# A hybrid attention block on one core: high parts over 128 partitions, and an order planned with the cost of changing partitions

## The chip, the core and the metric

The kernel runs on one core of a Trainium2 chip. The core has five engines that this text names as the profile does: PE (TensorE, matrix products), DVE (VectorE), ACT (ScalarE), POOL (GpSimd) and SP (SyncE, which issues most DMAs). Each works through its own queue in order; a semaphore holds an instruction until what it reads is there. The metric is the device time of one execution in microseconds, as the median of some runs. Before the change it is 288.33 us (three runs, 288.24 to 289.02).

## The reference

One decoder block over 512 tokens of width 1024. The normalised input goes through one combined projection into four head groups of four heads with 64 dimensions: forgetting attention (f), block-sparse attention (m), stick-breaking attention (s) and sliding-window attention with sinks (w). Each group's result is gated, and all of them go through one output projection onto the residual.

```python
hn = rms_norm(x, norm_gain)
proj = jnp.einsum('btd,de->bte', hn, w_in)
...
y = jnp.concatenate([from_heads(o_fox) * jax.nn.silu(fg),
                     from_heads(o_moba) * jax.nn.silu(mg),
                     from_heads(o_sb) * jax.nn.silu(sg),
                     from_heads(o_swa) * jax.nn.silu(wg)], axis=-1)
return x + jnp.einsum('bte,ed->btd', y, w_out)
```

In f, m and w the queries and keys are normalised per head and multiplied by a gain; in s they are not.

## The kernel before, in words

All matrix products are made of float32 values split into a high part (rounded to the type that PE reads fast, fp32r) and a low part (the rest). `hi_copy` (L138) makes the high part on ACT, `lo_part` (L142) the low part on DVE. A projection then has three products per step, high x high, low x high and high x low (`mm3`, L341 to L344).

Weights come in 39 chunks of up to 128 x 1024: sv, sqk, fvf, fqk, fg, sg, mqk, mv, mg, wg, wqkv, and eight of the output projection (o0 to o7). `advance` (L222) loads a chunk (three raw buffers), makes its high part on ACT and its low part on DVE, or on POOL in pieces of at most 260 columns where its number is in `POOL_LO`.

Scores of one head need q and k with 64 dimensions on partitions. Two heads lie in one 128-row tile, head 0 on rows 0 to 63, head 1 on rows 64 to 127. `q_pair` (L416) makes for each of the two heads a 128-row tile `qs`: the high part on the head's own rows ("mine") and the low part on the other half. `k_pair` (L428) makes a tile with two blocks of columns: in the first the high part of k on both halves, in the second the low part on the head's own rows and zeros on the other half. A score is then two products with the same weights (L511 and L512, or L507 in one). For f, m and w, q and k are first transposed on PE into PSUM (`qT`, `kT`, L455); for s they come from an SBUF tile (`sqk`). In w two heads share a k (`k_shared`), which is copied over all rows.

Each head goes on through a softmax or the stick-breaking sums on DVE and ACT (`pm`), transposes of the probabilities on PE (`pT`, L524), their high and low parts (`pth`, `ptl`), the product with v (L474, L475), and `lc` and `oc`, which add the two halves of that product (L487 on ACT, L488 on DVE); `lc` moves one half of the partitions to the other. The gate is multiplied on POOL (L493), and yh and yl are the parts for the output projection.

No engine's order is written out by hand. The program is recorded in a plain order; `_plan` (L1042) then plays all instructions through with costs per instruction (`_Step.cost`), and takes, of what can start first, the one with the lowest number: its place in the program plus the numbers in `TURN` for its kind. `PATIENCE` lets an engine wait that many ns for a lower number, `MARGIN` adds to a signal's way to an engine. `order_engines` (L1118) makes each engine keep that order. So each change of a cost moves instructions on all engines.

Of the kernel before, what the change touches and what calls it, by code (L numbers as in the profile page):

```python
# [40 lines left out]

RATE, OUTU = 4.54, 0.4

POOL_LO = {1, 4, 9, 10, 12, 15, 16, 19, 21, 23, 24, 30, 32, 34, 36, 37, 39}
PIECE = 260
DVE_SQ = {(1, 1), (2, 1), (3, 0), (3, 1)}

OCUT, WARM, WARM_GAPS = 2, 3, 8


TURN = {"xn": 215, "gate": 80, "qk": -250, "v": -68, "s": 14, "pt": -264, "ot": 322, "gap":
        100000, "y": 7, "fb": 5, "w": 81, "pv": -29, "oc": 258, "nat": -5, "proj": 65, "x": -110}
PATIENCE = {"Pool": 10, "PE": 21, "Activation": 29}

MARGIN = {"PE": 100, "Activation": 52}

LEAD = {"Pool": 120, "DVE": 0}


BOUNDS = list(range(17)) + [21, 27, 35, 46, 59, 77, 99, 128, 166, 216, 280, 363, 470]  # L60
# [18 lines left out]
def block_kernel(ctx, tc, x, xT, w_in, w_out, small, rel, out):  # L79
# [22 lines left out]
    def turn(name):  # L102
        def deco(f):
            def g(*a):
                with later(name):
                    return f(*a)
            return g
        return deco
# [24 lines left out]
    def pv(name):  # L133
        return ps.tile([P, 512], F32, tag="pv", name=name, bufs=1)
# [3 lines left out]
    def hi_copy(dst, src, scale=1.0):  # L138
        nc.scalar.activation(dst, src, AF.Copy if isinstance(scale, float) else AF.Identity,  # L139
                             scale=scale)  # L140

    def lo_part(dst, src, hi, scale=1.0):  # L142
        if isinstance(scale, float) and scale == 1.0:
            nc.vector.tensor_tensor(dst, src, hi.bitcast(F32), op=ALU.subtract)  # L144
        else:
            nc.vector.scalar_tensor_tensor(dst, src, scale, hi.bitcast(F32), op0=ALU.mult,
                                           op1=ALU.subtract)
# [5 lines left out]
    if WARM:  # L153
# [3 lines left out]
        pt = pv("warm")  # L157
# [64 lines left out]
    def advance():  # L222
# [23 lines left out]
        for a0 in range(0, ka, ka // cut):  # L246
            a = slice(a0, a0 + ka // cut)
            hi_copy(hv[:, a], rv[:, a])
            if n in POOL_LO:

# [13 lines left out]
    xn = [[sb.tile([P, 512], F32, tag="yh", name=f"x{t}{h}", bufs=9) for h in range(2)]  # L264
          for t in range(NT)]
    first = [load_raw() for _ in range(3)]
    for n in LOADS.split():
        k = int(n[1:] or 0)
# [135 lines left out]
    def sl(s, rows):  # L404
        return s if isinstance(s, float) else s[rows]
# [9 lines left out]
    @turn("qk")  # L415
    def q_pair(g, pr, pt):  # L416

        s = HD ** -0.5 if g == "s" else gain[g][:, 0:1]
        Q = []
        for h, (mine, other) in enumerate(((LO_, UP), (UP, LO_))):  # L420
            q = sb.tile([P, T], F32R, tag="qs", name=f"qs_{g}{pr}{h}", bufs=4)
            hi_copy(q[mine], pt[mine], sl(s, mine))
            lo_part(q[other], pt[mine], q[mine], sl(s, mine))
            Q.append(q)
        return Q

    @turn("qk")
    def k_pair(g, pr, pt):  # L428
        s = 1.0 if g == "s" else gain[g][:, 1:2]
        for h, (mine, other) in enumerate(((LO_, UP), (UP, LO_))):  # L430
            kh, kl = kk[pr, h][:, 0, :], kk[pr, h][:, 1, :]
            hi_copy(kh[mine], pt[mine], sl(s, mine))
            lo_part(kl[mine], pt[mine], kh[mine], sl(s, mine))
            hi_copy(kh[other], pt[mine], sl(s, mine))
        return [kk[pr, h] for h in range(2)]
# [289 lines left out]
    @turn("ot")  # L725
    def out_tile(t, c, ns, name):
        a = pj(name)[:, :c.stop - c.start]
        r = slice(t * P, (t + 1) * P)
        for m, n in enumerate(ns):
            yh, yl = ytile[eorder[n]]  # L730
            wh, wl = (v[:, 0, :] for v in oset.ch[n])
            mm3(a, yh[:, r], yl[:, r], wh[:, c], wl[:, c], m == 0, m == len(ns) - 1)
        return a
# [33 lines left out]
    a = [(sc if t == 3 else pj)(f"p_sv{t}")[:, :256] for t in range(NT)]  # L767
# [9 lines left out]
    for n in NORMS.split():  # L777
        if n == "a":
            advance()
        else:  # L780
            t, h = int(n) // 2, int(n) % 2
# [7 lines left out]
    for e in range(4):  # L789
        p = proj("sqk", e, 4, False, bank[SQK_BANKS[e]])  # L790
        a = sb.tile([P, T], F32, tag="wk", name=f"sqk{e}", bufs=3)
        nc.vector.tensor_tensor(a, p, rrow, op=ALU.mult)
        spair[e % 2].append((q_pair if e < 2 else k_pair)("s", e % 2, a))
# [52 lines left out]
    for t in range(NT):  # L846
        xr = wp.tile([P, D], F32, tag="raw", name=f"xr{t}", bufs=NRAW)
        nc.sync.dma_start(xr, x[t * P:(t + 1) * P, :])
        for half in range(2):
            c = slice(half * 512, (half + 1) * 512)  # L850
            a = out_tile(t, c, range(6), f"o1{t}{half}")
# [12 lines left out]
    for t in range(NT):  # L864
        for half in range(2):
            o = xres[t, half]
            cut = 512 // OCUT if t == NT - 1 and half else 512
            for c0 in range(0, 512, cut):
                c = slice(half * 512 + c0, half * 512 + c0 + cut)
                a = out_tile(t, c, range(6, 8), f"o2{t}{half}{c0}")  # L870
# [46 lines left out]
class _Step:  # L917
    def __init__(self, k, ins, slots):
        self.k, self.ins = k, ins
        self.eng = str(ins.engine).split(".")[-1]  # L920
        self.kind = type(ins).__name__[4:]
        self.func = str(getattr(ins, "func", "")).split(".")[-1]
        get = lambda l: [_Access(a.bass_ap, slots) for a in l or ()
                         if getattr(a, "bass_ap", None) is not None]
        self.reads, self.writes = get(ins.ins), get(ins.outs)
        self.ends = set()
        self.starts = set()
        self.extra = 0
        self.scan = (self.kind == "TensorScalarPtr" and len(self.reads) == 2
                     and self.reads[1].cols > 1 and self.reads[0].name == self.reads[1].name)  # L930

        streams = [a for a in self.reads if not a.psum
                   and (a.cols > 1 or self.writes[0].cols == 1)]
        self.port = self.eng == "Pool" and self.kind != "DMACopy" or self.eng == "DVE" and (
            len(streams) > 1 or self.kind in ("TensorScalarPtr", "TensorCopy")
            and len(streams) == 1 and not any(a.psum for a in self.reads + self.writes))
# [105 lines left out]
def _plan(steps, moved, held_back, turn, patience, margin):  # L1042

    at = {s.ins.name: s.k for s in steps}
    after = [[] for _ in steps]
    behind = [[] for _ in steps]
    open_ = [0] * len(steps)
    ready = [0.0] * len(steps)
    for s in steps:
        for k in s.ends:  # L1050
            after[k].append(s.k)
        starts = s.starts - s.ends
        if s.ins.name in held_back:
            starts.add(at[held_back[s.ins.name]])
        for k in starts:
            behind[k].append(s.k)
        open_[s.k] = len(s.ends) + len(starts)
    free, can, queue, rings = {}, {}, 0.0, []
    port = {"Pool": 0.0, "DVE": 0.0}
    other = {"Pool": "DVE", "DVE": "Pool"}  # L1060
    for s in steps:
        free[s.eng] = 600.0
        can.setdefault(s.eng, [])
        if not open_[s.k]:
            can[s.eng].append(s.k)
    prio = [s.k + sum(turn.get(n, 0) for n in moved.get(s.ins.name, ())) for s in steps]

    def start(e, k):

        t = max(free[e], ready[k])  # L1070
        if not steps[k].port:
            return t, t
        t += LEAD[e]
        return max(t, port[other[e]]), t

    plan = []
    for _ in steps:
        (t, _), e = min((start(e, k), e) for e in can for k in can[e])
        _, k, t = min((prio[k], k, start(e, k)[0]) for k in can[e]
                      if start(e, k)[0] <= t + patience.get(e, 0))  # L1080
        s = steps[k]
        t -= LEAD[e] if s.port else 0
        can[s.eng].remove(k)
        src, end = s.eng, t + s.cost()
        plan.append((s, t, end))
        free[s.eng] = end
        if s.port:
            port[s.eng] = end
        if s.kind == "DMACopy":

            big = max(a.cols * a.parts for a in s.reads + s.writes)
            if s.eng == "Pool":
                queue = max(t + 1680, queue) + big * 4 / 335.0
            else:
                if len(rings) > 7:
                    t = max(t, rings[-8] + 620)
                free[s.eng] = t + 475
                queue = max(t + 1130, queue) + big * 4 / 335.0
                rings.append(queue)
            src, end = "DMA", queue + 500  # L1100

        def release(ks, at, wait):
            for n in ks:
                e = steps[n].eng
                d = 0 if not wait else 900 if src == "DMA" else _LAT.get((src, e), 150)
                if wait and src != e:
                    d += margin.get(e, 0)
                ready[n] = max(ready[n], at + d)
                open_[n] -= 1
                if not open_[n]:  # L1110
                    can[e].append(n)

        release(after[k], end, True)
        release(behind[k], t, False)
    return plan


def order_engines(tc, slots, moved, held_back):  # L1118
    info = mybir.DependencyInfo(mybir.DependencyClass.NoSync, mybir.DependencyReason.DATA)
    last = {}  # L1120
    for s, _, _ in _plan(_steps(tc.nc, slots), moved, held_back, TURN, PATIENCE,
                         MARGIN):
        if s.eng in last:
# [30 lines left out]
```

## Time and profile before

| what | value |
| --- | --- |
| median of 3 runs | 288.33 us |
| profiled execution, its own time | 288.08 us |
| its span, first to last instruction | 286.3 us |
| PE busy | 280.3 us, 98% |
| DVE busy | 223.4 us, 78% |
| ACT busy | 203.1 us, 71% |
| POOL busy | 82.1 us, 29% |
| granted TensorE clock | 0.998 |

The span is one execution as the hardware profiler recorded it. An engine's share is the time in which one of its instructions was running. Matmuls overlap in PE's pipeline and their ends are modelled, so PE's share says little about how fast it works; the distance between two starts does. The chain of waits is followed back from the last instruction: at each step to what released it. An "idle before" in square brackets is the time in which the engine had nothing running, with the instruction that ended it.

### The profile page before, as it was taken

What the parts mean: (1) busy time and instruction counts of PE and PEld (TensorE: products, weight loads), DVE (VectorE), ACT (ScalarE), POOL (GpSimd) and SP (SyncE); (2) the same over time, 40 slices, a digit from 0 to 9 for tenths busy, and PEclk for the clock granted to TensorE, in tenths of its full rate; (3) what the DMA queues carried; (4) which work ended last, traced back from release to release, by engine and by line L of the source; (5) the groups of instructions that cost most, each with busy time, mean ns of one, the idle gap of its engine ahead of it and who ended that gap; (6) DMA issues with size and microseconds to landing.
All of it is one profiled execution on the core that took longest, in us unless ns stands there. A gap on an engine that the chain in (4) does not pass through costs nothing.

```text
span 286.3 us, 4633 instructions
## 1 busy us (share of the span) xinstructions
PE 280.3 (98%) x1529; PEld 235.3 (82%) x1529; DVE 223.4 (78%) x591; ACT 203.1 (71%) x476; POOL 82.1 (29%) x122
## 2 busy tenths in 40 slices
PE   8999999999999999999999999999999999999995
PEld 8988889888887878777799976778888788888884
DVE  3769287889899985878999787941897879998463
ACT  5874289967896964589998789697867887577100
POOL 5603052610046040357381000037103571001100
PEclk9999999999999999999999999999999999999999
DMA  7996342270024567351147041220230642400024
GB/s 248 349 396 187 110 150 73 73 222 0 0 76 130 169 175 194 87 163 44 39 116 217 7 140 39 84 100 0 77 92 0 236 152 92 166 2 0 2 112 181
DMA packets 19959, 33.64 MB, mean 117 GB/s; under 512 B 1616, under 2 KB 10068, under 8 KB 19808
## 3 DMA queue, kind: packets, MB, share of 16 engines
q1 hardware_dynamic: 19504, 32.96, 36.8%
q10 hardware_dynamic: 432, 0.39, 0.4%
q8 instruction: 12, 0.20, 0.3%
q14 instruction: 11, 0.09, 0.1%
HBM read 31.22 MB, written 4.22 MB: 124 GB/s over the span
## 4 chain that ended last, share of the span: by engine, by line
PE 63%; DVE 15%; ACT 15%; POOL 2%; DMA 2%; issue 2%; DVEq 0%
PE o L343 4%; PE o L344 4%; PE o L342 4%; ACT k L139 3%; PE p_fqk L342 2%; PE p_fqk L344 2%; PE p_sqk L343 2%; PE p_sqk L342 2%; PE p_wqkv L343 2%; PE p_fqk L343 2%; PE p_wqkv L342 2%; PE p_wqkv L344 2%; PE p_sqk L344 2%; POOL wl_o L254 2%; PE p_mqk L344 2%; PE p_mqk L343 2%
## 5 line engine op out<-in xcount | busy, mean ns | idle before, releaser
L254 POOL TENSOR_TENSOR wl_fqk<-raw_fqk,wh_fqk 128x260 fp32r<-128x260 f32 (+1 forms) x12 | 10.9, 932 | 23.0 <-ACT wh_fqk L139 23.0
L254 POOL TENSOR_TENSOR wl_sg<-raw_sg,wh_sg 128x256 fp32r<-128x256 f32 x8 | 7.8, 1009 | 24.3 <-ACT wh_sg L139 24.3
L597 DVE TENSOR_TENSOR_SCAN pm_s<-l 128x512 f32<-128x512 f32 (+3 forms) x16 | 13.7, 858 | 0.1
L493 POOL TENSOR_TENSOR oc_f<-oc_f,gate_f 128x512 f32<-128x512 f32 x2 | 2.6, 1287 | 38.9 <-ACT gate_f L760 38.9
L342 PE MATMUL p_mqk<-wh_mqk,xh 128*128 128x512 f32 x32 | 13.1, 408 | 0.0
L343 PE MATMUL p_mqk<-wl_mqk,xh 128*128 128x512 f32 x32 | 12.9, 404 | 0.0
L344 PE MATMUL p_mqk<-wh_mqk,xl 128*128 128x512 f32 x32 | 12.9, 402 | 0.0
L342 PE MATMUL p_fqk<-wh_fqk,xh 128*128 128x512 f32 x32 | 12.8, 400 | 0.0
L344 PE MATMUL p_fqk<-wh_fqk,xl 128*128 128x512 f32 x32 | 12.7, 398 | 0.0
L343 PE MATMUL p_wqkv<-wl_wqkv,xh 128*128 128x512 f32 x32 | 12.7, 397 | 0.0
L343 PE MATMUL p_fqk<-wl_fqk,xh 128*128 128x512 f32 x32 | 12.7, 401 | 0.0
L342 PE MATMUL p_wqkv<-wh_wqkv,xh 128*128 128x512 f32 x32 | 12.7, 396 | 0.0
L344 PE MATMUL p_wqkv<-wh_wqkv,xl 128*128 128x512 f32 x32 | 12.6, 394 | 0.0
L681 POOL TENSOR_SCALAR fxb<-fbc,scol 128x512 f32<-128x512 f32 (+3 forms) x16 | 9.6, 604 | 10.6 <-DVE nm_f L550 6.1
L343 PE MATMUL p_sqk<-xl,wh_sqk 128*128 128x512 f32 x32 | 12.5, 391 | 0.0
L342 PE MATMUL p_sqk<-xh,wh_sqk 128*128 128x512 f32 x32 | 12.5, 391 | 0.0
L344 PE MATMUL p_sqk<-xh,wl_sqk 128*128 128x512 f32 x32 | 12.3, 393 | 0.0
L493 POOL TENSOR_TENSOR oc_w<-oc_w,gate_w 128x512 f32<-128x512 f32 x2 | 2.6, 1292 | 32.5 <-DVE oc_w L488 32.5
L254 POOL TENSOR_TENSOR wl_o<-raw_o,wh_o 128x260 fp32r<-128x260 f32 (+1 forms) x8 | 6.7, 864 | 17.9 <-ACT wh_o L139 17.6
L144 DVE TENSOR_TENSOR ptl_m<-pT_m,pth_m 128x384 fp32r<-128x384 f32 (+3 forms) x16 | 7.4, 486 | 4.1 <-ACT pth_m L139 4.0
L552 ACT ACTIVATE pm_m<-pm_m,nm_m 128x512 f32<-128x512 f32 (+3 forms) x16 | 8.8, 553 | 2.3 <-DVE nm_m L550 2.3
L552 ACT ACTIVATE pm_w<-pm_w,nm_w 128x256 f32<-128x256 f32 (+1 forms) x16 | 7.6, 477 | 3.6 <-DVE nm_w L550 3.5
(357 smaller groups left out, 1115.2 us busy)
## 6 DMA issues: line engine op xcount, KB each, us to landing
raw_o<-in_w_out SPq DMA_DIRECT2D x8, 512.0 KB, 3.2
xT<-in_xT SPq DMA_DIRECT2D x8, 256.0 KB, 4.3
raw_sqk<-in_w_in SPq DMA_DIRECT2D x4, 512.0 KB, 6.0
x<-in_x SPq DMA_DIRECT2D x8, 256.0 KB, 5.8
raw_fqk<-in_w_in SPq DMA_DIRECT2D x4, 512.0 KB, 3.6
raw_mqk<-in_w_in SPq DMA_DIRECT2D x4, 512.0 KB, 3.7
raw_wqkv<-in_w_in SPq DMA_DIRECT2D x4, 512.0 KB, 3.6
xr<-in_x SPq DMA_DIRECT2D x4, 512.0 KB, 3.2
```

The lines of the kernel that those rows point to most:

```text
L139: nc.scalar.activation(dst, src, AF.Copy if isinstance(scale, float) else AF.Identity, scale=scale)
L144: nc.vector.tensor_tensor(dst, src, hi.bitcast(F32), op=ALU.subtract)
L254: nc.gpsimd.tensor_tensor(lv[q], rv[q], hv[q].bitcast(F32), op=ALU.subtract)
L342: nc.tensor.matmul(dst, ah, bh, start=first, stop=False)
L343: nc.tensor.matmul(dst, ah, bl, start=False, stop=False)
L344: nc.tensor.matmul(dst, al, bh, start=False, stop=last)
L493: nc.gpsimd.tensor_tensor(oc, oc, gates[e], op=ALU.mult)
L552: nc.scalar.activation(seg, seg, AF.Exp, scale=-1.0, bias=nm, accum_out=sm)
L597: nc.vector.tensor_tensor_scan(seg, l, l, 0.0, ALU.add, ALU.bypass)
L681: nc.gpsimd.tensor_scalar(b, bc[:, i * P:], -1.0, scol[:, i, h:h + 1], op0=ALU.mult, op1=ALU.add)
```

## The change

The high part of q is copied over all 128 rows, of both heads, and the low part is then written over the other half. The first high copy of k also goes over all 128 rows, and the second one overwrites the other half as before. The number of copies stays.

The planner gets two new costs. An instruction on ACT or DVE whose partitions (first partition and number, of its first operand and its result) differ from those of the one before it on its engine starts 133 or 113 ns after that one's end instead of at it. A PE instruction that is called by another engine less than 105 ns before PE is free, or later, ends up to 105 ns later. With these come new numbers in the tables: `TURN`, `PATIENCE`, `MARGIN`, and `POOL_LO`, which loses chunks 9, 12 and 23 (fqk0, fqk3, mg0) and gains 28, 29, 31, 35 and 38 (wqkv1, wqkv2, o0, o4, o7); 39 is no chunk.

```diff
-POOL_LO = {1, 4, 9, 10, 12, 15, 16, 19, 21, 23, 24, 30, 32, 34, 36, 37, 39}
+POOL_LO = {1, 4, 10, 15, 16, 19, 21, 24, 28, 29, 30, 31, 32, 34, 35, 36, 37, 38, 39}
...
-PATIENCE = {"Pool": 10, "PE": 21, "Activation": 29}
+PATIENCE = {"Pool": 10, "Activation": 53, "DVE": 4}
...
+SWITCH = {"Activation": 133, "DVE": 113}
+UNCOVERED = 105
...
-            hi_copy(q[mine], pt[mine], sl(s, mine))
+            hi_copy(q, pt, s)
             lo_part(q[other], pt[mine], q[mine], sl(s, mine))
...
-            hi_copy(kh[mine], pt[mine], sl(s, mine))
+            hi_copy(kh, pt, s)
             lo_part(kl[mine], pt[mine], kh[mine], sl(s, mine))
             hi_copy(kh[other], pt[mine], sl(s, mine))
...
+        self.rows = [(a.p0, a.parts) for a in (self.reads + self.writes)[::max(
+            1, len(self.reads))] if not a.dram] if self.eng in SWITCH else []
...
-        t = max(free[e], ready[k])
+        t = free[e]
+        if steps[k].rows and steps[k].rows != rows.get(e, steps[k].rows):
+            t += SWITCH[e]
+        t = max(t, ready[k])
...
+        if s.eng == "PE":
+            end += min(max(called[k] + UNCOVERED - free["PE"], 0), UNCOVERED)
+        if s.rows:
+            rows[s.eng] = s.rows
...
+                if wait and src != e:
+                    called[n] = max(called[n], at + d)
```

What this moves, at three places. On ACT, where q and k of group s are copied, before (qs_s00 is the q tile of pair 0, head 0; k01 the k tile of pair 0, head 1):

```order
L139 ACTIVATE wh_fqk0_550<-raw_fqk0_524 128x1024
L139 ACTIVATE qs_s00_445<-sqk0_443 64x512
L139 ACTIVATE qs_s01_448<-sqk0_443 64x512
L139 ACTIVATE qs_s10_478<-sqk1_476 64x512
L139 ACTIVATE qs_s11_481<-sqk1_476 64x512
L139 ACTIVATE k00_138<-sqk2_509 64x512 x2
L139 ACTIVATE k01_140<-sqk2_509 64x512 x2
L139 ACTIVATE k10_142<-sqk3_572 64x512 x2
L139 ACTIVATE k11_144<-sqk3_572 64x512 x2
L139 ACTIVATE v_f0_606<-p_fvf0_580,rx_129 128x4x64
```

and after:

```order
L144 ACTIVATE wh_fqk0_550<-raw_fqk0_524 128x1024
L144 ACTIVATE qs_s00_445<-sqk0_443 128x512
L144 ACTIVATE qs_s01_448<-sqk0_443 128x512
L144 ACTIVATE qs_s10_478<-sqk1_476 128x512
L144 ACTIVATE qs_s11_481<-sqk1_476 128x512
L144 ACTIVATE k00_138<-sqk2_509 128x512
L144 ACTIVATE k01_140<-sqk2_509 128x512
L144 ACTIVATE wh_fqk1_562<-raw_fqk1_536 128x1024
L144 ACTIVATE k00_138<-sqk2_509 64x512
L144 ACTIVATE k01_140<-sqk2_509 64x512
L144 ACTIVATE k10_142<-sqk3_569 128x512
L144 ACTIVATE k11_144<-sqk3_569 128x512
```

The copies are 128 rows high but for the second ones of k, and a weight copy (wh_fqk1) stands between the first and the second copy of k00.

On PE, where the first scores of group m stand (p_mg0 and p_mg1 are tiles of a gate's projection, qT_m1 the transposed q of the second pair of heads, s_m00 and s_m01 the scores of head 0), before:

```order
L343 MATMUL p_mg0_2198<-xl1_134,wh_mg1_1902 128x512
L344 MATMUL p_mg0_2198<-xh1_132,wl_mg1_1903 128x512
L511 MATMUL s_m00_2345<-k00_138,qs_m00_2308 128x512
L512 MATMUL s_m00_2345<-k00_138,qs_m00_2308 128x512
L455 MATMUL qT_m1_2320<-ident_82,nat_m0_1612 128x128
L455 MATMUL qT_m1_2320<-ident_82,nat_m1_1710 128x128
L455 MATMUL qT_m1_2320<-ident_82,nat_m2_1794 128x128
L455 MATMUL qT_m1_2320<-ident_82,nat_m3_1921 128x128
L511 MATMUL s_m01_2354<-k00_138,qs_m00_2308 128x384
L512 MATMUL s_m01_2354<-k00_138,qs_m00_2308 128x384
L342 MATMUL p_mg0_2198<-xh1_132,wh_mg1_1902 128x512
```

and after:

```order
L349 MATMUL p_mg0_2189<-xh1_132,wl_mg1_1894 128x512
L347 MATMUL p_mg1_2249<-xh0_131,wh_mg0_1881 128x512
L348 MATMUL p_mg1_2249<-xl0_133,wh_mg0_1881 128x512
L460 MATMUL qT_m1_2317<-ident_82,nat_m0_1606 128x128
L460 MATMUL qT_m1_2317<-ident_82,nat_m1_1704 128x128
L460 MATMUL qT_m1_2317<-ident_82,nat_m2_1788 128x128
L460 MATMUL qT_m1_2317<-ident_82,nat_m3_1912 128x128
L516 MATMUL s_m00_2342<-k00_138,qs_m00_2305 128x512
L517 MATMUL s_m00_2342<-k00_138,qs_m00_2305 128x512
L516 MATMUL s_m01_2351<-k00_138,qs_m00_2305 128x384
L517 MATMUL s_m01_2351<-k00_138,qs_m00_2305 128x384
L349 MATMUL p_mg1_2249<-xh0_131,wl_mg0_1882 128x512
```

The four transposes now stand ahead of the head's first scores, one matmul of the gate later.

On POOL, toward the end (wl_o1 is the low part of chunk o1, wo5 that of o5, oc_m1 the gating of m's second pair), before:

```order
L254 TENSOR_TENSOR wl_o1_2819<-raw_o1_2464,wh_o1_2818 128x260 x3
L254 TENSOR_TENSOR wl_o1_2819<-raw_o1_2464,wh_o1_2818 128x244
L254 TENSOR_TENSOR wl_o3_2846<-raw_o3_2816,wh_o3_2845 128x260 x3
L254 TENSOR_TENSOR wl_o3_2846<-raw_o3_2816,wh_o3_2845 128x244
L254 TENSOR_TENSOR wo5_3060<-raw_o5_2843,wo5_3060 128x260 x3
L254 TENSOR_TENSOR wo5_3060<-raw_o5_2843,wo5_3060 128x244
L254 TENSOR_TENSOR wo6_3066<-raw_o6_2858,wo6_3066 128x260
L493 TENSOR_TENSOR oc_m1_2892<-oc_m1_2892,gate_m1_2295 128x512
L254 TENSOR_TENSOR wo6_3066<-raw_o6_2858,wo6_3066 128x260 x2
L254 TENSOR_TENSOR wo6_3066<-raw_o6_2858,wo6_3066 128x244
L493 TENSOR_TENSOR oc_w0_3208<-oc_w0_3208,gate_w0_2406 128x512
```

and after:

```order
L259 TENSOR_TENSOR wl_o3_2846<-raw_o3_2816,wh_o3_2845 128x260 x3
L259 TENSOR_TENSOR wl_o3_2846<-raw_o3_2816,wh_o3_2845 128x244
L259 TENSOR_TENSOR wl_o4_2861<-raw_o4_2831,wh_o4_2860 128x260 x3
L259 TENSOR_TENSOR wl_o4_2861<-raw_o4_2831,wh_o4_2860 128x244
L259 TENSOR_TENSOR wo5_3063<-raw_o5_2843,wo5_3063 128x260 x3
L498 TENSOR_TENSOR oc_m1_2895<-oc_m1_2895,gate_m1_2292 128x512
L259 TENSOR_TENSOR wo5_3063<-raw_o5_2843,wo5_3063 128x244
L259 TENSOR_TENSOR wo6_3069<-raw_o6_2858,wo6_3069 128x260 x3
L259 TENSOR_TENSOR wo6_3069<-raw_o6_2858,wo6_3069 128x244
L259 TENSOR_TENSOR wo7_3075<-raw_o7_3061,wo7_3075 128x260 x3
L259 TENSOR_TENSOR wo7_3075<-raw_o7_3061,wo7_3075 128x244
L498 TENSOR_TENSOR oc_w0_3214<-oc_w0_3214,gate_w0_2403 128x512
```

The low parts of o4 and o7 are now split here, o4 ahead of oc_m1, o7 behind it; o0 is too, further up. Two more places in words: on PE the first scores of s stand behind one matmul of p_fvf1 before and behind 14 after, and between the transposes kT_w0 and the first scores of w there are 7 matmuls of the output projection before and 9 after.

## Rows read from the trace of the kernel before

**Rows 1.** The page's first lines: the span, and PE's busy time, its share of the span and its instructions.

```profile
span 286.3 us, 4633 instructions
...
PE 280.3 (98%) x1529; PEld 235.3 (82%) x1529; DVE 223.4 (78%) x591; ACT 203.1 (71%) x476; POOL 82.1 (29%) x122
```

**Rows 2.** The page's chain that ended last, its shares by engine.

```profile
PE 63%; DVE 15%; ACT 15%; POOL 2%; DMA 2%; issue 2%; DVEq 0%
```

**Rows 3.** The timeline of PE and DVE around 168 us, where group m begins: start, duration (both us), engine, line, operation, tiles, and the idle time before it with what ended it.

```profile
168.56 0.39 PE L511 MATMUL s_m<-k,qs_m 128*128 128x512 f32 x1
168.79 0.40 PE L512 MATMUL s_m<-k,qs_m 128*128 128x512 f32 x1
169.34 0.63 PE L455 MATMUL qT_m<-ident,nat_m 128*128 128x128 f32 x4 [0.15 <-DVE qs_m L146]
...
167.71 0.69 DVE L488 TENSOR_TENSOR oc_f<-o_f,lc_f 64x512 f32<-64x512 f32 x1
168.44 0.76 DVE L146 SCALAR_TENSOR_TENSOR qs_m<-qT_m,small,qs_m 64x512 fp32r<-64x512 f32 x1
```

**Rows 4.** The timeline of PE at the first and the last of its late starts, columns as in rows 3: at 42.9 and 242.5 us, and the first and the last of the small ones, at 5.8 and 259.3.

```profile
42.21 0.28 PE L342 MATMUL p_fvf<-wh_fvf,xh 128*128 128x260 f32 x1
42.93 0.68 PE L511 MATMUL s_s<-k,qs_s 128*128 128x512 f32 x2 [0.44 <-ACT k L139]
43.44 0.29 PE L343 MATMUL p_fvf<-wl_fvf,xh 128*128 128x260 f32 x1
...
242.12 0.39 PE L342 MATMUL o<-wh_o,yh_s 128*128 128x512 f32 x1
242.55 0.36 PE L511 MATMUL s_w<-k,qs_w 128*128 128x256 f32 x1
...
5.54 0.39 PE L342 MATMUL p_sv<-wh_sv,xh 128*128 128x256 f32 x1
5.76 0.28 PE L343 MATMUL p_sv<-wl_sv,xh 128*128 128x256 f32 x1
...
259.04 0.39 PE L475 MATMUL o_w<-ptl_w,v_w 128*128 128x256 f32 x1
259.26 0.28 PE L474 MATMUL o_w<-pth_w,v_w 128*128 128x256 f32 x1
```

**Rows 5.** The timeline of ACT at the first copies of group w: a copy of 64 rows from partition 0, then one of 128 rows from partition 0.

```profile
233.18 0.69 ACT L139 ACTIVATE qs_w<-qT_w,small 64x512 fp32r<-64x512 f32 x1
233.76 0.67 ACT L139 ACTIVATE k<-kT_w,small 128x512 fp32r<-128x512 f32 x1
```

**Rows 6.** The timeline of ACT around 196 us: lc_m moves 64 rows to the other half, the others have 128 rows.

```profile
195.47 0.59 ACT L487 ACTIVATE lc_m<-o_m 64x512 f32<-64x512 f32 x1
196.09 0.63 ACT L139 ACTIVATE yh_s<-oc_s 128x512 fp32r<-128x512 f32 x1
196.63 1.14 ACT L139 ACTIVATE yh_f<-oc_f 128x512 fp32r<-128x512 f32 x2
```

**Rows 7.** The timeline of ACT at the q and k copies of group s, and the weight copy that follows.

```profile
38.98 2.58 ACT L139 ACTIVATE qs_s<-sqk 64x512 fp32r<-64x512 f32 x4
41.59 1.94 ACT L139 ACTIVATE k<-sqk 64x512 fp32r<-64x512 f32 x3
...
47.19 1.05 ACT L139 ACTIVATE wh_fqk<-raw_fqk 128x1024 fp32r<-128x1024 f32 x1
```

**Rows 8.** The timeline of PE at the first transposes of m's probabilities.

```profile
173.94 0.39 PE L343 MATMUL p_mg<-xl,wh_mg 128*128 128x512 f32 x1
174.50 0.30 PE L524 MATMUL pT_m<-ident,pm_m 128*128 128x128 f32 x1 [0.17 <-DVE qs_m L146]
...
176.94 0.39 PE L342 MATMUL p_mg<-xh,wh_mg 128*128 128x512 f32 x1
177.54 0.33 PE L524 MATMUL pT_m<-ident,pm_m 128*128 128x128 f32 x1 [0.22 <-ACT k L139]
```

**Rows 9.** The timeline of PE at the first scores of w.

```profile
234.30 0.40 PE L342 MATMUL o<-wh_o,yh_s 128*128 128x512 f32 x1
234.80 0.47 PE L511 MATMUL s_w<-k,qs_w 128*128 128x256 f32 x2
235.12 0.39 PE L343 MATMUL o<-wl_o,yh_s 128*128 128x512 f32 x1
```

**Rows 10.** Groups of DVE's instructions by shape: low parts of whole weight chunks; busy us and mean ns of one.

```profile
L144 DVE TENSOR_TENSOR wl_mqk<-raw_mqk,wh_mqk 128x1024 fp32r<-128x1024 f32 x3 | 4.3, 1423 | 0.3 <-ACT wh_mqk L139 0.3
L144 DVE TENSOR_TENSOR wl_wqkv<-raw_wqkv,wh_wqkv 128x1024 fp32r<-128x1024 f32 x3 | 3.7, 1224 | 0.9 <-ACT wh_wqkv L139 0.9
```

**Rows 11.** Busy time of each engine (PE, PEld, DVE, ACT, POOL, with the number of instructions) in one stretch, then the clock, the DMA share and GB/s.

```profile
162.00:191.00 29.00, 28.34 (x148) 22.37 (x148) 23.05 (x55) 24.28 (x49) 0.82 (x1) 1.00 0.32 91
```

**Rows 12.** The timeline of POOL: a chunk's low part in four pieces, and the first pieces of wo with the idle time before them.

```profile
219.20 3.83 POOL L254 TENSOR_TENSOR wl_o<-raw_o,wh_o 128x260 fp32r<-128x260 f32 x4 [17.58 <-ACT wh_o L139]
...
230.49 3.53 POOL L254 TENSOR_TENSOR wo<-raw_o,wo 128x260 fp32r<-128x260 f32 x5 [4.31 <-ACT wo L139]
```

**Rows 13.** The timeline of DVE and POOL around 119.9 us, and the group of the same DVE product for group f.

```profile
119.88 0.66 DVE L289 TENSOR_TENSOR rum<-rum,rmm 128x8 f32<-128x8 f32 x1
...
118.36 2.84 POOL L254 TENSOR_TENSOR wl_mv<-raw_mv,wh_mv 128x256 fp32r<-128x256 f32 x4 [14.72 <-ACT wh_mv L139]
...
L289 DVE TENSOR_TENSOR ruf<-ruf,rmf 128x8 f32<-128x8 f32 x4 | 0.5, 156 | 0.0
```

More of the change, by code (lines that the diff above doesn't have):

```diff
@@ L48 @@
 OCUT, WARM, WARM_GAPS = 2, 3, 8
-TURN = {"xn": 215, "gate": 80, "qk": -250, "v": -68, "s": 14, "pt": -264, "ot": 322, "gap":
-        100000, "y": 7, "fb": 5, "w": 81, "pv": -29, "oc": 258, "nat": -5, "proj": 65, "x": -110}
-PATIENCE = {"Pool": 10, "PE": 21, "Activation": 29}
-MARGIN = {"PE": 100, "Activation": 52}
+TURN = {"xn": 248, "gate": 62, "qk": -554, "v": -52, "s": 14, "pt": -266, "ot": 445, "gap":
+        100000, "y": -13, "fb": -567, "w": 55, "pv": -34, "oc": 258, "nat": -1, "proj": 65, "x":
+        46}
+PATIENCE = {"Pool": 10, "Activation": 53, "DVE": 4}
+MARGIN = {"PE": 100, "Activation": 52, "DVE": 44}
 LEAD = {"Pool": 120, "DVE": 0}
+SWITCH = {"Activation": 133, "DVE": 113}
+UNCOVERED = 105
 BOUNDS = list(range(17)) + [21, 27, 35, 46, 59, 77, 99, 128, 166, 216, 280, 363, 470]
@@ L1048, in _plan @@
     ready = [0.0] * len(steps)
+    called = [0.0] * len(steps)
     for s in steps:
@@ L1059, in _plan @@
     port = {"Pool": 0.0, "DVE": 0.0}
+    rows = {}
     other = {"Pool": "DVE", "DVE": "Pool"}
```

## The prediction

> **What bounds the kernel now.** I read the engine shares first. PE is busy 280.3 of 286.3 us [rows 1], so only time in which PE is not fed can be won. The profiled execution took 288.08 us, so 1.78 us lie around its span; it stands 0.25 us under the median of 288.33. Then the chain of waits: 63% of it is PE, 15% each DVE and ACT [rows 2], so the chain leaves PE often, although PE shows hardly any idle time. PE's timeline says why: matmuls of 512 columns start 0.23 us apart and are drawn 0.39 long [rows 3], so a pause of up to 0.16 us does not show as idle. I therefore read starts, not busy time. Against a pace of 0.227 us for 512 columns, 0.12 for 256 or 260, 0.17 for 384 and 0.11 for a transpose, 15 of PE's starts after 5.4 us come late by more than 0.12 us, 4.4 us together. The first is the score at 42.93, 0.72 behind a 260-column matmul, the last the one at 242.55, 0.43 behind one of 512 [rows 4]. Another 27 are late by 0.06 to 0.12 us, 2.5 us together, the first at 5.76, the last at 259.26 [rows 4]; many follow a late start at once, as the two scores at 42.93 (512 and 384 columns, 0.40 by the pace) take 0.51 up to 43.44. So about 7 us of PE's time can be won, no more: 281.
>
> **The change part by part.** *1. The copies.* Copying the high part over 128 rows costs the engine nothing by itself: a 64x512 copy out of PSUM takes 0.69 us, a 128x512 one 0.67 [rows 5]. What changes is the step between neighbours. On ACT, lc_m (which moves one half of the partitions to the other) ends at 196.06 and yh_s starts at 196.09; yh_s ends at 196.72 and yh_f starts at 196.63 [rows 6]. So neighbours with the same first partition, in and out, overlap by 0.09, others stand 0.03 apart: a change costs 0.12 us. Counted in ACT's order there are 73 such changes before and 54 after; on DVE 53 and 52. The q copies no longer make one, the second k copy still does. So at most 19 x 0.12 = 2.3 us of ACT time go, and none where ACT waited there anyway.
>
> The Trainium skill, in "ScalarE: Activation LUTs" (What ACT_TABLE_LOAD costs), says that ACTIVATEs in a row overlap by about 93 ns and makes no exception; by it this part would win nothing. The trace agrees only for equal first partitions [rows 6].
>
> *2. The new order.* The planner now adds 133 or 113 ns where the partitions change and up to 105 where PE is called late, and the turns are new. Four places can be followed.
>
> First scores of s (42.2 us): 13 more matmuls of p_fvf1 stand ahead, 13 x 0.12 = 1.56 us, against a wait of 0.60 and 0.11 behind it. But the chain grows too. The q copies start at 38.98, 0.65 apart [rows 7]; at 0.54 the four end 0.45 us sooner, at 41.14. Then two full k copies (to 42.2), wh_fqk1 (1.05 less the overlap, to 43.2), and only then the second half of k00, to 43.9, 1.0 later than before. DVE's low part of q, behind wl_fqk0 of 1.2 us, ends near 41.9, in time. PE comes at 42.21 + 0.12 + 1.56 = 43.9 as well. With some 0.2 us for the signal I take 0.5 of the 0.71.
>
> Second transposes of m (168.8): qT_m1 waited for DVE's low part of q and started 0.33 late [rows 3]. It now stands behind 15 matmuls instead of 16, ahead of the scores, so PE comes at 168.8 instead of 169.0; but the DVE addition oc_f of 0.69 has gone from between the two low parts of q, which brings the second one's end from 169.2 to 168.5. I take 0.44, the pause and the 0.11 that a late start costs behind it.
>
> First transposes of m's probabilities: late by 0.33 and 0.38 [rows 8] while ACT alternated k, q and exponentials; it now does most exponentials of the first head together, ahead of the second pair's k. I take 0.3 of the 0.7.
>
> First scores of w: 0.28 late and 0.08 behind it [rows 9]; two more 512-column matmuls stand ahead, 0.45. I take 0.36.
>
> Sum 1.6 us, in which part 1 is contained. The other pauses, some 4 us in 35 places, can't be followed singly. The nearest row for one is the restart of 0.11 [rows 4]: twenty fewer would give 2.2, twenty more cost 2.2. PE goes from one stream to another 546 times in the order before and 530 times after; that speaks for neither side, and I take 0.
>
> *3. The low parts of the weights.* fqk0, fqk3 and mg0 go from POOL to DVE (12 pieces); wqkv1, wqkv2, o0, o4 and o7 from DVE to POOL (20 pieces). One is 1.22 us on DVE when undisturbed [rows 10]: DVE gets 3.7 us more before 160 us and 6.1 less after. The cover: between 162 and 191 us POOL is busy 0.8 of 29 us, so the two wqkv chunks fit; DVE is busy 23.1 there [rows 11]. Around 230 POOL sat idle 4.3 us ahead of wo, and one such chunk took it 3.8 [rows 12], so o4 fits. If that cover fails, oc_m1 leaves POOL about 1 us late, ACT's yh_m1 with it, and PE meets it at the last products of o100. I put the part at 0, between a gain of 1 us (DVE relieved where it is three quarters busy) and a loss of 3 (third rival).
>
> Sum on the profiled execution: 288.08 - 1.6 = 286.5; on the median's footing 286.7.
>
> **The rivals.** *No change, about 288.2.* For it: each start that comes sooner makes the next wait visible, as at the s place, where 1.56 us of cover met a chain grown by 1.0. And the planner counts too much: it takes a change in the number of rows for a change of partitions. On ACT the copy of 64 rows from partition 0 ends at 233.87 and the 128-row one behind it starts at 233.76 [rows 5], so this costs nothing. The new order holds 9 such places on ACT and 26 on DVE; if DVE behaves alike, 26 x 0.113 = 2.9 us exist in the plan alone, and if that takes half of the 1.6 back the time is 287.5. Against it: the true changes in the plan are 106, three times as many, and the plan of before had none of them.
>
> The Trainium skill's "VectorE: DVE Perf Modes" (Two Vector instructions with no wait between them) has this as a rule: an instruction is held back only where a start quadrant differs from that of the last read or write; the count of rows plays no part. By that rule the plan is up to 2.9 us late on DVE, which is the 287.5 above. The row agrees, on ACT [rows 5].
>
> *A larger win, about 284.8.* If plan and chip now agree to a tenth of a microsecond, half of all late starts go, 3.5 of 7 us. For it: nearly 9 us of ACT's time (73 x 0.12) that the plan of before left out. Against it: many late starts arise where a signal comes within 0.1 us of PE, and single durations of one kind scatter by as much (1224 to 1423 ns in rows 10).
>
> *Slower, about 290.3.* POOL and DVE get into each other's way. At 119.88 a DVE product on 8 columns takes 0.66 us instead of 0.16, while POOL splits mv [rows 13]: 0.5 us a meeting. The place is 166 to 190 us, where eight pieces enter a time that was free of POOL and DVE works for the scores of m, and again o0 and o4 up to 233. Twenty pieces of 0.5 are 10 us of DVE against the 6.1 it is spared, 3.9 net; with PE fed by DVE there, half of it reaches PE and the gain is gone as well: 288.3 + 2. It decides from about twelve meetings (6.0 against 6.1), and from sixteen PE loses its first 0.9 us. Against it: most of DVE's work there reads PSUM or one stream.
>
> **How the numbers follow.** The forecast, 285.3 to 287.4, gets 0.55; no change, 287.5 to 289.2, gets 0.22; the larger win, below 285.3, 0.11; slower, above 289.2, 0.12. A difference under 0.3% (0.86 us) can't be told from none here, so faster means under 287.47: 0.55 + 0.11 = 0.66; within 0.22; slower 0.12. The range 284.6 to 289.0 leaves out about half of the larger win, the slower case and the edge of no change, 2 in 10 together; the likeliest case alone has 285.3 to 287.4.
>
> **What would show it.** Right: ACT's q copies of 128x512 start about 0.09 before their neighbour's end where ACT does not wait; the first score of s is late by 0.2 at most and qT_m1 not at all; late starts on PE sum to about 5.3 us; DVE is busy some 6 us less after 160 us. Wrong: the same sum of late starts at other places (no change); small DVE instructions of 0.6 us beside POOL's pieces between 166 and 190, and more late starts there (slower). The copies alone did nothing if what ACT gains lies in front of waits for DVE's low parts.

## The result, and the profile after

The changed kernel takes 284.89 us (median of four: 285.07, 290.99, 284.02, 284.71) beside 288.28 for the kernel before, measured on the same chip. The ratio is 0.9868, 95% interval 0.9836 to 0.9899: 3.8 us less, where 1.6 was forecast, and within 0.1 us of the 284.8 that the larger win was given. Five more rounds gave 0.9861 (0.9831 to 0.9891). A ratio leaves out executions more than 1.5% above the fastest, of the changed kernel three of ten (289.3 to 291.4 us); the last group of experiments asks what happens in them. The profiled execution took 285.07.

The page of the changed kernel: its span and busy times, and the chain by engine.

```profile
span 283.0 us, 4658 instructions
...
PE 277.7 (98%) x1529; PEld 236.2 (83%) x1529; DVE 221.0 (78%) x589; ACT 202.1 (71%) x476; POOL 86.7 (31%) x130
...
PE 95%; DMA 2%; DVE 1%; ACT 0%; ACTq 0%; issue 0%
```

Against [rows 1] PE is again busy 98%, of a span 3.3 us shorter. The chain tells more: PE had 63% of it [rows 2] and now has 95%. The path hardly leaves PE any more. Late starts are reckoned with the prediction's paces: a start is late by what it comes after the sum of the paces since the last late one, and all of more than 0.02 us count. After 10 us they sum to 7.15 us before and 3.42 after; those over 0.12 us go from 15 to 5. Ahead of 10 us they grow, from 0.37 to 1.34.

PE in the changed kernel, at the places of [rows 4], [rows 3] and [rows 9]: the first scores of s, the second transposes of m, the first scores of w.

```profile
44.49 0.28 PE L348 MATMUL p_fvf<-wl_fvf,xh 128*128 128x260 f32 x1
44.60 0.65 PE L516 MATMUL s_s<-k,qs_s 128*128 128x512 f32 x2
45.09 0.28 PE L349 MATMUL p_fvf<-wh_fvf,xl 128*128 128x260 f32 x1
...
168.71 0.40 PE L348 MATMUL p_mg<-xl,wh_mg 128*128 128x512 f32 x1
168.94 0.60 PE L460 MATMUL qT_m<-ident,nat_m 128*128 128x128 f32 x4
...
234.09 0.28 PE L512 MATMUL s_w<-k,qs_w 128*128 128x256 f32 x1
234.20 0.40 PE L347 MATMUL o<-wo,yh_m 128*128 128x512 f32 x1
234.44 0.40 PE L348 MATMUL o<-wo,yh_m 128*128 128x512 f32 x1
234.81 0.50 PE L349 MATMUL o<-wo,yl_m 128*128 128x512 f32 x1
```

The s scores start 0.11 behind the matmul ahead of them and cost 0.09 over the pace (0.71 before); qT_m1 starts 0.23 behind its neighbour, on the pace. The matmul on yl_m at 234.81 is new among the late: 0.37 behind its neighbour, 0.14 late, and 0.11 behind it.

ACT at the copies of s, to compare with [rows 7], and at the start of the program, with PE there.

```profile
39.71 2.17 ACT L144 ACTIVATE qs_s<-sqk 128x512 fp32r<-128x512 f32 x4
41.79 1.14 ACT L144 ACTIVATE k<-sqk 128x512 fp32r<-128x512 f32 x2
42.83 1.04 ACT L144 ACTIVATE wh_fqk<-raw_fqk 128x1024 fp32r<-128x1024 f32 x1
43.90 2.47 ACT L144 ACTIVATE k<-sqk 64x512 fp32r<-64x512 f32 x4
...
6.71 0.42 ACT L144 ACTIVATE wh_sv<-raw_sv 128x256 fp32r<-128x256 f32 x1 [1.16 <-DMA raw_sv<-in_w_in]
...
7.79 0.39 PE L347 MATMUL p_sv<-wh_sv,xh 128*128 128x256 f32 x1 [0.80 <-ACT xh L144]
```

Four q copies take 2.17 us instead of 2.58: 0.52 from one to the next, where they stood 0.65 apart. At the start PE loses 0.96 us: the second xh copy stands on ACT behind the third wh_sv copy, and that one's transfer landed a microsecond later than in the profile of before.

### The profile page after: what moved, and what is told of

It reads as the page before. It is cut to its first block, busy times and chain, and to the rows that moved or that the text cites. A ratio compares the mean times of both kernels' runs of the same rounds, so it can differ in the third digit from the quotient of the medians.

```text
span 283.0 us, 4658 instructions
## 1 busy us (share of the span) xinstructions
PE 277.7 (98%) x1529; PEld 236.2 (83%) x1529; DVE 221.0 (78%) x589; ACT 202.1 (71%) x476; POOL 86.7 (31%) x130
## 4 chain that ended last, share of the span: by engine, by line
PE 95%; DMA 2%; DVE 1%; ACT 0%; ACTq 0%; issue 0%
PE o L349 5%; PE o L347 5%; PE o L348 5%; PE p_fqk L348 3%; PE p_fqk L349 3%; PE p_wqkv L348 3%; PE p_mqk L349 3%; PE p_wqkv L347 3%; PE p_mqk L348 3%; PE p_mqk L347 3%; PE p_fqk L347 3%; PE p_wqkv L349 3%; PE p_sqk L348 3%; PE p_sqk L349 3%; PE p_sqk L347 3%; DMA raw_sv<-in_w_in 2%
## 5 line engine op out<-in xcount | busy, mean ns | idle before, releaser
L259 POOL TENSOR_TENSOR wl_o<-raw_o,wh_o 128x260 fp32r<-128x260 f32 (+1 forms) x16 | 12.8, 828 | 20.1 <-ACT wh_o L144 20.1
L259 POOL TENSOR_TENSOR wl_wqkv<-raw_wqkv,wh_wqkv 128x260 fp32r<-128x260 f32 (+1 forms) x12 | 8.6, 753 | 28.9 <-PE pT_m L529 28.2
L149 DVE TENSOR_TENSOR ptl_m<-pT_m,pth_m 128x512 fp32r<-128x512 f32 (+3 forms) x16 | 7.5, 488 | 7.4 <-ACT pth_m L144 7.4
L604 ACT ACTIVATE pm_s<-pm_s 128x512 f32<-128x512 f32 (+3 forms) x16 | 7.3, 464 | 7.0 <-DVE pm_s L603 6.9
L347 PE MATMUL p_sv<-wh_sv,xh 128*128 128x256 f32 x32 | 9.0, 289 | 0.8 <-ACT xh L144 0.8
```

What stands on the lines that cost most here:

```text
L259: nc.gpsimd.tensor_tensor(lv[q], rv[q], hv[q].bitcast(F32), op=ALU.subtract)
L347: nc.tensor.matmul(dst, ah, bh, start=first, stop=False)
L604: nc.scalar.activation(seg, seg, AF.Exp)
```

## The experiments

Each kernel ran beside the kernel before on its chip. "Written order" means that the planner is replaced by the list of instructions that it had made for one of the two kernels, so that nothing moves but what the diff shows:

```diff
-    for s, _, _ in _plan(_steps(tc.nc, slots), moved, held_back, TURN, PATIENCE,
-                         MARGIN):
+    steps = _steps(tc.nc, slots)
+    for s in (steps[k] for k in WRITTEN):
```

**The copies and the order apart.** Theory A: the win is the order, the copies are worth nothing without it. Theory B: the copies carry it. A third kernel takes back the low parts, and the changed kernel ran again.

full_old, written order of before:

```diff
-            hi_copy(q[mine], pt[mine], sl(s, mine))
+            hi_copy(q, pt, s)
...
-            hi_copy(kh[mine], pt[mine], sl(s, mine))
+            hi_copy(kh, pt, s)
```

> Order of before, instruction for instruction, with the copies of q and of the first k over 128 rows. Theory A (the win is the order, the copies are worth nothing without it): 287.8 to 288.5 us, the late starts of PE as before, the s pause at 42.9 us shorter by at most 0.4. Theory B (the copies carry the win, 19 changes of partition by 0.12 us of ACT): 286.2 us or below.

half_new, written order of the changed kernel, with the same lines the other way round:

> Order of the changed kernel, instruction for instruction, with the copies of 64 rows of before. Theory A: 284.5 to 285.5 us, at most 0.7 above the changed kernel, which is what the s place may lose (its copies are 0.5 us later). Theory B: 286.5 us or above, as the 19 changes come back on ACT.

old_low, the changed kernel with

```diff
-POOL_LO = {1, 4, 10, 15, 16, 19, 21, 24, 28, 29, 30, 31, 32, 34, 35, 36, 37, 38, 39}
+POOL_LO = {1, 4, 9, 10, 12, 15, 16, 19, 21, 23, 24, 30, 32, 34, 36, 37, 39}
```

> The changed kernel with the POOL_LO of before; the planner and the other tables are those of the changed kernel and plan anew (400 of 1455 rows of PE's order differ). If the move of low parts is worth nothing, as the prediction took it: 284.3 to 285.7 us. If DVE's relief of 6 us after 160 us carries part of the win: 286 us or above, with more late starts of PE behind DVE after 160 us.

> The changed kernel once more, beside the others. Both theories: about 284.5 us. If the pause of 0.96 us ahead of p_sv at 6.7 us belongs to the order, it stands in this profile too; if the landing of one raw_sv transfer scatters, the third wh_sv copy starts up to 1 us earlier here and the span is up to 1 us shorter.

Measured, as a ratio to the kernel before: full_old 0.9964 (0.9950 to 0.9977), half_new 0.9915 (0.9892 to 0.9938), old_low 0.9905 (0.9882 to 0.9928), again 0.9861. On 288.3 us that is -1.0 for the copies alone, -2.5 for order and low parts without them, -4.0 for all: the parts add up within the intervals, and both theories fall. The copies are worth 1.0 in the old order (0.7 to 1.4) and about 1.6 in the new one (uncertain by 1.1).

PE and ACT in half_new at the scores of s show where the copies work, with the order held:

```profile
39.76 2.58 ACT L144 ACTIVATE qs_s<-sqk 64x512 fp32r<-64x512 f32 x4
...
44.53 0.28 PE L348 MATMUL p_fvf<-wl_fvf,xh 128*128 128x260 f32 x1
45.44 0.68 PE L516 MATMUL s_s<-k,qs_s 128*128 128x512 f32 x2 [0.63 <-ACT k L144]
```

The four copies take 2.58 again, and PE comes 0.91 behind the matmul ahead, 0.79 over the pace. In full_old the pause of s shrinks likewise, from 0.71 to 0.18 with the restart. So it was the copies that filled this place; the 13 matmuls moved ahead of it only kept step with the longer chain.

The same two profiles part the other late starts. The three largest that the prediction did not follow are these in the kernel before (the second row of each pair, 0.27, 0.45 and 0.31 late):

```profile
91.52 0.39 PE L512 MATMUL s_s<-k,qs_s 128*128 128x512 f32 x1
92.02 0.44 PE L511 MATMUL s_s<-k,qs_s 128*128 128x384 f32 x1
...
103.14 0.39 PE L342 MATMUL p_mqk<-wh_mqk,xh 128*128 128x512 f32 x1
103.82 0.39 PE L507 MATMUL s_s<-k,qs_s 128*128 128x256 f32 x1 [0.29 <-DVE fS L662]
...
123.02 0.39 PE L343 MATMUL p_mqk<-wl_mqk,xh 128*128 128x512 f32 x1
123.56 0.50 PE L511 MATMUL s_f<-k,qs_f 128*128 128x512 f32 x1
```

In full_old the last two stay (0.28 at 103.3 us, 0.31 at 123.1), and so do those of qT_m1 (0.31) and of the first of the two late transposes of m's probabilities (0.34). The first of the three, the second of the two transposes and the first scores of w are no longer late by 0.12 there. In half_new none of all these is. So, by one profile of each, the order takes all seven without the copies, and the copies alone take three of them. In the changed kernel no start from 60 to 129 us is late by more than 0.09; the first score of f comes right behind its transposes:

```profile
122.60 0.60 PE L460 MATMUL qT_f<-ident,nat_f 128*128 128x128 f32 x4
122.96 0.47 PE L516 MATMUL s_f<-k,qs_f 128*128 128x512 f32 x1
```

old_low stands 1.3 us above the changed kernel, with an uncertainty of 1.1 from the two intervals, and its plan differs in more than the low parts. The other way round, new_low (POOL_LO of the changed kernel in the kernel before, its planner and tables kept):

> The kernel before with the POOL_LO of the changed kernel alone; its planner, tables and half copies stay (429 rows of PE's order differ). If POOL's taking over of low parts is a gain by itself, as old_low has it (1.2 us): 286.8 to 287.4 us. If it is a gain only together with the new order: 288.2 us or above.

It took 290.30 us, ratio 1.0069 (1.0042 to 1.0096): 2 us slower, the second case and more. The same exchange of pieces is a loss with one planner and a gain with the other, which plan anew around it; one place of the loss is shown below.

**The planner's two costs.**

```diff
-SWITCH = {"Activation": 133, "DVE": 113}
+SWITCH = {}
```

> The changed kernel with SWITCH empty: the copies, low parts and tables stay, the planner no longer charges a change of partitions (547 of 1455 rows of PE's order differ). If that cost is what brought the order of the changed kernel near the chip: 285.3 to 287 us, more late starts on PE behind ACT. If the order is as good without it (chance, or its 35 miscounted places eat what it gives): 283.8 to 285.2 us.

```diff
-UNCOVERED = 105
+UNCOVERED = 0
```

> The changed kernel with UNCOVERED = 0: the planner no longer charges up to 105 ns for a late start of PE (446 of 1455 rows of PE's order differ). If that cost carries the win: 285.3 to 287 us, more late starts of 0.06 to 0.12 us. If not: 283.8 to 285.2 us.

```diff
-        self.rows = [(a.p0, a.parts) for a in (self.reads + self.writes)[::max(
+        self.rows = [a.p0 for a in (self.reads + self.writes)[::max(
```

> The changed kernel with the planner's rows compared by the first partition alone, so the 35 places where only the number of rows changes cost nothing in the plan (374 of 1455 rows of PE's order differ). If these miscounted places spoil the order: 283.0 to 284.0 us. If they are harmless, or the tables are fitted to them: 284.2 to 286.5 us.

no_switch: 290.48 us, 1.0071 (1.0048 to 1.0093), 6 us above the changed kernel and slower than before. no_late: 0.9888 (0.9865 to 0.9911), 0.7 above, which the intervals don't tell from none. start_part: 0.9883 (0.9858 to 0.9907), no better. With these tables the charge for a change of partitions is what the order needs; that it is also charged where only the number of rows changes does no harm that can be measured. All three keep tables fitted to the full set of costs, so this is the worth of a cost with these tables, not by itself, and no run has the new tables with the old planner or the other way round.

PE's waits of no_switch after 10 us (total us, times, longest):

```profile
PE o L349 <- DVE yl_m L149: 1.5, 1, 1.5
PE o L347 <- DVE part L863: 0.9, 1, 0.9
PE s_s L516 <- DVE pm_s L603: 0.6, 1, 0.6
PE p_mv L347 <- DVE nat_m L385: 0.4, 1, 0.4
PE o_f L479 <- DVE oc_f L493: 0.3, 1, 0.3
PE qT_f L460 <- DVE qs_f L151: 0.2, 1, 0.2
```

and the whole answer for the changed kernel:

```profile
PE s_f L512 <- DVE nm_f L555: 0.4, 1, 0.4
```

Between 10 and 220 us the late starts of no_switch sum to 6.6 us, those of the changed kernel to 2.4 and of the kernel before to 5.9: pauses all over the program, not at one place. Behind 220 us they sum to 3.7 beside 1.0; 1.7 of that is the wait for yl_m, which the last group explains, so not all of the 6 us is pauses of the kind that the charge was made for.

**The pause at the start.** swap, written order of the changed kernel, the second xh copy ahead of the third wh_sv copy on ACT:

```diff
 ACTIVATE wh_sv0<-raw_sv0 128x256
+ACTIVATE xh0<-xT1,small 128x512
 ACTIVATE wh_sv0<-raw_sv0 128x256
-ACTIVATE xh0<-xT1,small 128x512
```

> Order of the changed kernel, but on ACT the second copy xh0 (of xT_92) ahead of the third copy of wh_sv0, which waits for its transfer. Theory: the pause ahead of p_sv (0.96 and 0.67 us in two profiles) is that xh0 queued behind a late transfer; it goes to under 0.3, and the executions end 0.3 to 0.8 us sooner, 283.6 to 284.2 us. Rival: PE then waits for the transfer itself twelve matmuls on: no change, 284.4 us.

0.9854 (0.9828 to 0.9879): no change. In its profile ACT waits 0.73 us for the transfer of xT itself, and PE loses 0.22 at this place and 0.73 five matmuls on. Across the profiles ACT's third wh_sv copy starts at 5.69 (before), 6.71 (after), 6.46 (again), 6.22 (full_old), 5.79 (old_low) and 7.25 us (new_low), with the same transfers in the same order ahead of it. The first, fourth and last have the order of before on ACT here, the others that of the changed kernel. So this microsecond is scatter of the first transfers and belongs to neither order.

**The shut-out of yl_m.** The profiled execution of half_new took 293.0 us. DVE, POOL and PE there, at the low part of m's second pair, then the clock in stretches of 2 us (columns as in rows 11):

```profile
234.99 5.43 DVE L149 TENSOR_TENSOR yl_m<-oc_m,yh_m 128x512 fp32r<-128x512 f32 x1
...
233.64 6.24 POOL L259 TENSOR_TENSOR wo<-raw_o,wo 128x244 fp32r<-128x244 f32 x9
...
240.48 0.79 PE L349 MATMUL o<-wo,yl_m 128*128 128x512 f32 x1 [4.06 <-DVE yl_m L149]
...
236.00:238.00 2.00, 0.42 (x2) 0.00 (x0) 2.00 (x1) 1.76 (x7) 2.00 (x4) 1.00 0.47 188
238.00:240.00 2.00, 0.00 (x0) 0.00 (x0) 2.00 (x1) 0.00 (x0) 1.88 (x3) 0.86 0.00 0
240.00:242.00 2.00, 1.52 (x5) 1.33 (x6) 1.94 (x6) 0.16 (x1) 0.00 (x0) 0.50 0.00 1
```

yl_m reads two streams from the buffer memory, as POOL's pieces do. It is called while POOL is in the second of nine pieces that stand back to back, and ends half a microsecond after the last. PE waits 4.06 us, and the granted clock falls to 0.50 (1.2 GHz) and stays there for more than 6 us, to past 246. In the profiled execution of the changed kernel the same nine pieces let it in:

```profile
233.41 1.34 DVE L149 TENSOR_TENSOR yl_m<-oc_m,yh_m 128x512 fp32r<-128x512 f32 x1
...
232.08 6.83 POOL L259 TENSOR_TENSOR wo<-raw_o,wo 128x244 fp32r<-128x244 f32 x9
```

The profile of start_part, an execution of 290.66 us, has the 5.43 once more, and in new_low and no_switch, where five pieces stand there, yl_m takes 2.75 and 2.80:

```profile
233.62 5.43 DVE L149 TENSOR_TENSOR yl_m<-oc_m,yh_m 128x512 fp32r<-128x512 f32 x1
```

```profile
239.17 2.75 DVE L144 TENSOR_TENSOR yl_m<-oc_m,yh_m 128x512 fp32r<-128x512 f32 x1
...
237.89 3.48 POOL L254 TENSOR_TENSOR wo<-raw_o,wo 128x244 fp32r<-128x244 f32 x5
```

In the profiled execution of new_low PE loses 1.69 us there; whether the other executions of it do isn't shown. The test: let POOL wait for yl_m. peek and peek2 put one small POOL instruction into the written order, peek ahead of the nine pieces, peek2 behind two of them:

```diff
         lo_part(yl, oc, yh)
+        if e == ("m", 1):
+            nc.gpsimd.tensor_scalar(peek, yl[:, :1].bitcast(F32), 1.0, None, op0=ALU.mult)
```

> Order of the changed kernel; after oc_m1, POOL first reads one column of yl_m1, so its nine pieces of wo wait until DVE has written yl_m1. Theory: where an execution of the changed kernel or of half_new takes over 289 us, DVE's yl_m1 is shut out by the nine pieces (5.43 us instead of 1.3 in the profile of half_new); then yl_m1 takes 0.6 to 0.7 here and none of six executions is over 287; the median is within 0.5 of the changed kernel's 284.4. Rival: those executions have nothing to do with yl_m1; then about two of six are over 289 here too.

> As peek, but POOL reads the column of yl_m1 two pieces later (behind the last piece of wo5 and the first of wo6), so the transfer of xr, which takes the buffer that wo5's last piece frees, is issued at about 232 as in the changed kernel and not 2.3 us later. Theory: peek's 1.7 us over the changed kernel came from that transfer, and the executions over 289 us from the shut-out of yl_m1; then yl_m1 takes at most 0.8, no execution is over 287, and the median is 284.0 to 284.8. Rival: two pieces ahead are enough to shut DVE out (1.3 us more), or the delay of wo7 costs as before: 285.5 us or above.

> peek2 once more, for more executions of it. Theory (the executions over 289 us come from yl_m1 being shut out): again none of six over 287, so none of eighteen with peek and peek2, where about one in four of the changed kernel was; median 284.2 to 285.5 us. Rival (they come by chance of the chip): one or two of six over 289.

peek: 285.77 to 286.52 us, 0.9928 (0.9910 to 0.9946). peek2: 0.9875 (0.9850 to 0.9901), then 0.9879 (0.9858 to 0.9900). None of the 17 executions is above 286.6, where the written order without it (the changed kernel, half_new, swap) has 7 of 22 at 289 or more; by chance alone that would come about once in ninety times. Only two of the long executions were profiled (half_new, start_part), and both have the 5.43. DVE and POOL in peek2:

```profile
232.00 0.69 DVE L149 TENSOR_TENSOR yl_m<-oc_m,yh_m 128x512 fp32r<-128x512 f32 x1
...
230.66 1.41 POOL L259 TENSOR_TENSOR wo<-raw_o,wo 128x244 fp32r<-128x244 f32 x2
232.78 0.21 POOL L506 TENSOR_SCALAR peek<-yl_m 128x1 f32<-128x1 f32 x1 [0.70 <-DVE yl_m L149]
232.95 5.05 POOL L259 TENSOR_TENSOR wo<-raw_o,wo 128x260 fp32r<-128x260 f32 x7
```

yl_m takes 0.69. peek stands 1.8 us above the changed kernel by the ratios, not within 0.5; its profile has the reason, a transfer that the expectation had left out:

```profile
237.74 0.69 DVE L867 TENSOR_TENSOR part<-o,xr 128x512 f32<-128x512 f32 x1 [1.20 <-DMA xr<-in_x]
...
238.49 0.49 PE L347 MATMUL o<-wh_o,yh_s 128*128 128x512 f32 x1 [0.69 <-DVE part L867]
```

The residual xr is loaded into the buffer that wo5's last piece frees; held back by 2.3 us, that piece held the transfer back, DVE's addition and PE's next tile. peek2 lets it go first. It stands about 0.4 us above the changed kernel by the ratios, which the intervals don't tell from none; over all executions its mean is 285.1 (11) beside 286.3 (10) for the changed kernel. It is the version to keep.

One more meeting of the two engines explains the largest late start that the changed kernel has left after 10 us, 0.58 at 144.72. DVE, POOL and PE there, and DVE and POOL in again, which runs the same instructions in the same order:

```profile
143.49 0.70 DVE L298 SCALAR_TENSOR_TENSOR r0m<-rum,r0m 128x8 f32<-128x8 f32 x1
...
143.43 0.73 POOL L259 TENSOR_TENSOR wl_mg<-raw_mg,wh_mg 128x256 fp32r<-128x256 f32 x1
...
144.02 0.28 PE L348 MATMUL p_mv<-wl_mv,xh 128*128 128x256 f32 x1
144.72 0.38 PE L512 MATMUL s_f<-k,qs_f 128*128 128x256 f32 x1 [0.42 <-DVE nm_f L555]
```

```profile
143.21 0.15 DVE L298 SCALAR_TENSOR_TENSOR r0m<-rum,r0m 128x8 f32<-128x8 f32 x1
...
143.23 0.74 POOL L259 TENSOR_TENSOR wl_mg<-raw_mg,wh_mg 128x256 fp32r<-128x256 f32 x1
```

Of the seven profiles with this order, r0m starts 0.05 to 0.06 us behind POOL's piece in three (the changed kernel, half_new, peek2_more), takes 0.70 or 0.71, and PE is late by 0.58 or 0.59. In the other four it starts 0.02 ahead of the piece, takes 0.15 or 0.16, and the score is on time.

## Why the prediction was right, and where it was wrong

*The bound* held: most of the time came out of PE's late starts. 3.7 us of them went after 10 us, 1.0 were added ahead of it, and PE's last matmul ends 3.31 us sooner; of the other 0.6, 0.24 is an earlier first projection (5.30 instead of 5.54), the rest lies in starts less than 0.02 late and in the pace. By the two sizes that the prediction counted (over 0.06 us) they sum to 4.1 us, where it said 5.3.

*Part 1, the copies.* The cost of a change, 0.12 us, and the bound of 2.3 us held: the q copies step 0.13 closer, and full_old shows 1.0 us of time for it. The sum of 1.6 had this part "contained" in it, with no price of its own; it is worth 1.0 without any of the rest. The Trainium skill's 93 ns of overlap, in "ScalarE: Activation LUTs" (What ACT_TABLE_LOAD costs), would have given nothing for it; full_old and the kernel before, one order with and without the copies, contradict that, and so do the changed kernel and half_new.

*Part 2, four places.* 1.6 of 2.2 was taken, 1.9 came: s gave 0.62 (0.5 said), qT_m1 all of its 0.44 (its second low part of q ended at 168.47, 168.5 said), the transposes of m's probabilities the whole 0.7 instead of 0.3, w its 0.36, though the wait for yl_m returns 0.25 beside it.

*The step that failed* is the last paragraph of part 2: "The other pauses, some 4 us in 35 places, can't be followed singly ... and I take 0." They gave 1.8 us. Two things were wrong in it. It sized them by the restart of 0.11; but ten of the 15 starts over 0.12 us lay outside the four places, 2.4 us together, the largest at 103.82 (0.45), 123.56 (0.31) and 92.02 (0.27), and all three are gone. And it took the sign as open because the count of changes of stream spoke for neither side; no_switch shows what should have spoken: without the charge the late starts up to 220 us are back at 6.6 us, above the 5.9 of the kernel before. The larger win's reason, "nearly 9 us of ACT's time" that the plan of before left out, fits this, and so does its size: half of the late starts went, as it said. How much of it the charge does and how much the new numbers in the tables is open, as no run parts the two.

*Part 3, low parts.* It was put at 0, between a gain of 1 and a loss of 3. About 1.3 was gained in the new order (uncertain by 1.1), 2.0 lost in the old one: the bounds hold within that uncertainty, but it is not nothing. DVE is busy 2.4 us less, as counted. After 160 us it is spared 3.5, not 6: 166 to 190 us spares it 2.4 (17.07 beside 19.42), and 190 to 219 us, 21.05 beside 17.77, takes more than that back, as other work moved there.

*The rivals.* No change: the places that the planner counts too much did no harm that start_part can show. Slower: from 166 to 190 us no DVE instruction of the changed kernel takes 0.2 us more than the shortest of its kind, though POOL is busy 10.2 us there. Meetings at 197.4 and 200.0 us (yl_s 1.77 instead of 0.71, yl_f 1.01 instead of 0.68) made no start of PE late. But one at 143.5 costs PE 0.58, and at the end of the rival's second place, just past 233, the mechanism does decide, not by twelve meetings of 0.5 us but by one of 4, in about a third of the executions. The rival had the mechanism and the engines, and the wrong shape.

## What to carry to other kernels

List every late start of the bound engine over a tenth of a microsecond with its cause before calling the rest noise, and when a planner learns a cost that it lacked, look for the gain at all places where that cost was missing, not only at the few that can be followed. Where POOL runs a queue of two-operand pieces back to back, don't let a DVE instruction with two operands from the buffer memory fall due behind its first piece if PE waits for it; one small POOL instruction that reads the result first is enough, put where it holds back no piece that frees a buffer. Time a kernel over many executions: such a lock shows in some and not in others.

## What the runs showed of the hardware

A DVE instruction with two streams from the buffer memory, called while POOL works off a queue of such instructions, waited for the whole queue: 5.43 us behind nine pieces, 2.75 and 2.80 behind five, instead of 0.69. The Trainium skill, "SBUF — State Buffer" (SBUF: two separate sides), says that DVE and POOL share a pair of ports under a lock which whoever starts first holds for its whole instruction. The runs agree: r0m on 8 columns took 0.15 us where it started 0.02 ahead of a POOL piece, and 0.70 where it started 0.05 to 0.06 behind. But behind a queue the lock passed from one POOL instruction to the next without letting DVE in. In other executions with the same queue DVE did get in after a part of a piece or one (0.81 to 1.34 us). What decides between the two is open: behind nine pieces it was shut out when called 1.33 and 1.35 us after the queue began, and let in when called 1.33 to 1.86 us after. What DVE's wait then does to PE was seen too: idle from 236.4 to 240.5 us in half_new, with the granted clock at 1.00, 0.86 and 0.50 in the three stretches from 236 to 242 us.
